# A hybrid Hyena/attention/expert block in fp32: absolute values of the filters written to SBUF, the input projection's casts and evictions early in the program's order, the third sine ahead of the products with the norm

## The chip, the core and the metric

The kernel runs on one core of one Trainium2 chip. The metric is the time of one execution in device microseconds (us); for a version it is the median of several runs.

## What is computed

One encoder layer on a sequence of L = 1024 tokens with D = 1024 channels, batch 1, all in fp32. The reference, cut to what matters here:

```python
mod = silu(c) @ w_ada + b_ada                  # sh1, sc1, gt1, sh2, sc2, gt2
h = rms_norm(x, g_mix) * (1 + sc1) + sh1
z = h @ w_in + b_in                            # -> hyena v, x1, x2 | q | k | v | branch gates
# filters: a three-layer sine MLP 33 -> 64 -> 64 -> 64 on the position, then w4
hdn = sin(fr[0] * (pos @ w1 + b1)); hdn = sin(fr[1] * (hdn @ w2 + b2)); hdn = sin(fr[2] * (hdn @ w3 + b3))
f = (hdn @ w4) * exp(-t * abs(deltas)); f = f / (sum(abs(f), axis=0) + EPS)
y = v                                          # hyena: short 3-tap convolution of z first
for o in range(2):
    y = gates[o] * (bidir_fftconv(y, f[:, o, 0], f[:, o, 1]) + fb[o] * y)
o = softmax(rope(norm(q)) @ rope(norm(k)).T) @ v       # 8 heads, 2 of them for keys and values
x = x + gt1 * ((sigmoid(g_hy) * (y @ w_hy_out) + sigmoid(g_at) * (o @ w_att_out)) @ w_out)
x = x + gt2 * expert_choice_ffn(rms_norm(x, g_ffn) * (1 + sc2) + sh2)   # 16 SwiGLU experts
```

## The kernel before

**Arithmetic.** TensorE multiplies in a fast fp32 form ("fp32r"), so a product of full accuracy is three products of high and low parts, a_h b_h + a_h b_l + a_l b_h: `mm3`, L145 to L147. A high part is a cast on ScalarE, a low part a subtraction on VectorE. For a block of weights that pair is `wsplit`: cast wh at L140, residual wl at L141, from a raw tile wr that SyncE loads.

**Stages.** Times are those of the profiled execution.

- 0 to 60 us, the head. ScalarE and VectorE compute the norm of x and the three sine layers; `sine` is the range reduction on VectorE (L226 to L232, tile wf), `sin` the table function on ScalarE. VectorE multiplies the eight tiles of x by the norm; this is "the products with the norm". `by_rows` (L246) is the product of silu(c) with w_ada for shift1, and `columns` turns its row into columns with two copies (L252, tile z) and 16 tiny products (L255). The third layer's sine stands behind the products with the norm, its casts (tiles Hs, sh) behind it. All this runs in `in_order()`, which chains the instructions of each engine in the order of the code. At its end `shifted` (L361, L363) applies scale and shift to x, and casts and residuals make hT, the input of the input projection (L367, L369, L373).
- 60 to 117 us, the filters: `filters(0)`, `filters(1)`. For each, the weights w4 are cast (L269) and reduced to the residual (L270). Eight times: four products per filter tile into PSUM tile pS (L280), times the decay (VectorE, L284; the decay itself is ScalarE's L274), the absolute value with a running sum on ScalarE (L285), whose result goes back into pS and isn't read, and then the normalisation (L290) and a store to DRAM, k_s.
- 117 to 358 us, `spectra(0)` and `spectra(1)`. `plane` loads a plane of a filter (tile xg, L441), `tokens` transposes it on TensorE (L447), `split2` makes high and low parts (L428, L429: sh, sl), and `dft` multiplies it by constants that `load_const` fetches on the queue of POOL (tile dc, L434). An 8-point FFT on VectorE (`fft8`) combines the planes.
- Then rotary q, k and v, written to DRAM (QT_s, KT_s, V_s), and `hyena_in(0)` to `hyena_in(11)`: the projection blocks of the hyena inputs with the three taps (L417) and a store.
- 358 to 635 us, the two convolutions, chained through generators: forward transform, product with the spectrum, `inverse` (casts Zh, Zl at L671, L672), gate; in the second one the result is transposed and gated (L717) and stored to y_s.
- From 635 us attention: `scores` (products, maximum L793, exponential L795), `turned` (transposes L804, casts L808, L809: ph, pl), `values`, and as filler between them `hyena_out`, which loads y_s (tile yq, L850), splits it (L852, L853: yh, yl) and multiplies by w_hy_out. Then merge and output projection (to about 1050 us), routing and the experts (to the end).

**The input projection** is 34 blocks of 128 columns, `win_block(m)`: 0 to 11 hyena, 12 to 17 q, k, v (their eviction is L553, tile ge), 18 to 33 gates. Each is 48 products in two halves, into PSUM tile pM, and an eviction `evac` on ScalarE.

**What sets the order.** Each engine carries out its queue in order. The queues are filled by a list scheduler: among instructions whose producers it holds done, the one with the lowest priority number is next. The number is a counter, `tc.cur_priority`, that grows with the code, so code that is written early is placed early. `lane(n)` gives the projection's products numbers from 1,000,000 n on, which makes them fillers: they are taken where nothing else is ready. Their casts, residuals and evictions had numbers of their place in the code.

**Buffers.** Tiles of one tag share a number of buffers: f4 9, z4 3, Z 4 (decays, zt, Zh, Zl, QT), dc 3, xg 2, H 2 (here the times t01, later the loaded spectra), wr, wh, wl, sh, sl, wf, ge and yq 2 each; PSUM pS, pT, pM 2 each. A tile can be written when the last reader of that buffer is done. SyncE issues most transfers, POOL those of dc and the first loads of QT, KT, V.

Of the kernel before, what the change touches and what calls it, by code (L numbers as in the profile page):

```python
# [51 lines left out]
def block(tc, xT, cols_d, rows_d, mlp_d, w4_d, dfc_d, idf_d, rope_d, wada_d, win_d, why_d, watt_d, wout_d, wr_d,  # L52
# [133 lines left out]
    def mixer_head():  # L186
# [11 lines left out]
        def z4(shape=(128, 1024), dt=F32):  # L198
            return wk.tile(list(shape), dt, name="z4", tag="z4", bufs=3)
# [65 lines left out]

        def filters(o):

            w4h, w4l = z4(dt=F32R), z4(dt=F32R)
            nc.scalar.copy(w4h, w4r[o])  # L269
            nc.vector.tensor_sub(w4l, w4r[o], w4h)  # L270
            sums = rn[:, o * 8:o * 8 + 8].rearrange("p (b r) -> p b r", r=2)
            for b in range(4):
                dec = wk.tile([128, 1024], F32, name="dec", tag="Z", bufs=4)
                nc.scalar.activation(dec, t01b, AF.Exp, scale=col("ndel", b))  # L274
                ts = []
                for dr in range(2):
                    m = dr * 4 + b
                    ps = pS()
                    for hf in range(2):
                        mm(ps[:, hf], w4h[:, m * 128:(m + 1) * 128], Hs[hf], start=True, stop=False)  # L280
                        mm(ps[:, hf], w4l[:, m * 128:(m + 1) * 128], Hs[hf], start=False, stop=True)
                    t = f4([128, 1024])
                    pf = ps.rearrange("p a b -> p (a b)")
                    nc.vector.tensor_mul(t, pf, dec)  # L284
                    nc.scalar.activation(pf, t, AF.Abs, accum_out=sums[:, b, dr:dr + 1])  # L285
                    ts.append(t)
                nc.vector.tensor_scalar(sums[:, b], sums[:, b], EPS, None, op0=ALU.add)
                nc.vector.reciprocal(sums[:, b], sums[:, b])
                for dr, t in enumerate(ts):
                    nc.scalar.activation(t, t, AF.Copy, scale=sums[:, b, dr:dr + 1])  # L290
                    nc.sync.dma_start(k_s[o, dr, b], t.rearrange("p (q t) -> p q t", q=8))
# [8 lines left out]
        with in_order():  # L300
# [30 lines left out]
                                    rr[:, q:q + 1].to_broadcast([128, 128]), ident)  # L331
            for k in range(4, 8):
                adaln(acc, stage[1][k], k)
            for k in range(8):
                nc.vector.tensor_mul(xt[k], xt[k], rb.rearrange("p a b -> p (a b)"))
            prow = [pT([1, 512]) for hf in range(2)]
# [2 lines left out]
                if k == 2:  # L339
                    mod_cols(acc, 1, pM)  # L340
            nc.vector.scalar_tensor_tensor(G1, modc[:, 8:16], 1.0, col("g_mix", 0, 8), op0=ALU.add, op1=ALU.mult)
            h = sine(p3, "b3", "f3")
            sin(h)
            up, low = slice(64, 128), slice(0, 64)
            t = w2("sh", dt=F32R)
            Hs += [hsp.tile([128, 512], F32R, name=f"Hs{hf}") for hf in range(2)]
            nc.scalar.copy(Hs[0][low], h[low])
            nc.scalar.copy(t[up], h[up])
            nc.vector.tensor_sub(Hs[0][up], h[low], Hs[0][low])
            nc.vector.tensor_sub(Hs[1][up], h[up], t[up])  # L350
            first = wsplit(first)
            pg = columns(prow)
            nc.scalar.copy(Hs[1][low], h[up])
            nc.vector.tensor_add(modc[:, 0:8], pg, col("b_ada", 0, 8))
            sx.close()
            hpool = hx.enter_context(tc.tile_pool(name="hT", bufs=1, side="right", reuse_waits="tile"))
# [9 lines left out]
            for k in range(0, 8, 2):  # L366
                nc.scalar.copy(hTh[k], xt[k])  # L367
                shifted(k + 1)
                nc.scalar.copy(hTh[k + 1], xt[k + 1])  # L369
                if k < 6:  # L370
                    shifted(k + 2)
                for i in (k, k + 1):
                    nc.vector.tensor_sub(hTl[i], xt[i], hTh[i])  # L373
        filters(0)
        if "Hs" in dbg:
            for hf in range(2):
# [7 lines left out]


        def win_block(m, evac, n=0):
            wh, wl = first if m == 12 else wsplit(wload(win_d[m]))

            def step(ps, sl, k):
                ks = slice(k * 128, k * 128 + 128)  # L390
                mm3(ps, (wh[:, ks], wl[:, ks]), (hTh[k][:, sl], hTl[k][:, sl]), k == 0, k == 7)
            halves = [slice(hf * 512, hf * 512 + 512) for hf in range(2)]
            if m == 12:

                ps = [pM() for sl in halves]
                for k in range(8):
                    for hf, sl in enumerate(halves):
                        step(ps[hf], sl, k)
                for hf, sl in enumerate(halves):
                    evac(ps[hf], sl)  # L400
                return
            for sl in halves:
                ps = pM()
                with lane(n) if n else ExitStack():
                    for k in range(8):
                        step(ps, sl, k)
                evac(ps, sl)

        def hyena_in(m, n=0):
            z = z4([128, 8, 128])  # L410
# [19 lines left out]
            return h, l  # L430

        def load_const(src):
            t = w2("dc", [128, 2, 256], F32R, 3)
            nc.gpsimd.dma_start(t, src)  # L434
            return t


        def plane(src, q, spare=False):

            t = z4([128, 4, 128]) if spare else w2("xg", [128, 4, 128])  # L440
            nc.sync.dma_start(t, src[:, :, q].rearrange("b p c -> p b c"))  # L441
            return t

# [1014 lines left out]
```

## Time and profile before

| | |
|---|---|
| median of 3 runs | 2263.3 us (2262.97 to 2269.51) |
| profiled execution | 2261.93 us, its span 2260.1 us |
| mean granted TensorE clock | 0.979 |
| PE (TensorE matmul) | 2129.1 us busy, 94% of the span, 10090 instructions |
| PEld (weight loads, beside PE) | 1686.4 us, 75% |
| DVE (VectorE) | 1886.3 us, 83% |
| ACT (ScalarE) | 1303.9 us, 58% |
| POOL (GpSimd) | 118.2 us, 5% |
| HBM | 538.60 MB read, 65.01 MB written |

The span goes from the first to the last instruction; 1.8 us of the execution lie around it. Shares are averages over very different stages: over half of the span is the experts, which the change doesn't touch. A row of a group reads: line, engine, operation, output <- inputs, partitions x elements; then busy time and mean ns, and the idle time of the engine just before them with what ended it. A row of the timeline begins with start and length in us; in square brackets stands the wait before it and what released it. A row of the table of stages gives each engine's busy time and number of instructions in a stretch; PEclk is TensorE's granted clock as a share of the full one.

### The profile page before, as it was taken

What the parts mean: (1) busy time and instruction counts of PE and PEld (TensorE: products, weight loads), DVE (VectorE), ACT (ScalarE), POOL (GpSimd) and SP (SyncE); (2) the same over time, 40 slices, a digit from 0 to 9 for tenths busy, and PEclk for the clock granted to TensorE, in tenths of its full rate; (3) what the DMA queues carried; (4) which work ended last, traced back from release to release, by engine and by line L of the source; (5) the groups of instructions that cost most, each with busy time, mean ns of one, the idle gap of its engine ahead of it and who ended that gap; (6) DMA issues with size and microseconds to landing.
All of it is one profiled execution on the core that took longest, in us unless ns stands there. A gap on an engine that the chain in (4) does not pass through costs nothing. (4 is left out here: it accounts for less than half of the span.)

```text
span 2260.1 us, 26964 instructions
## 1 busy us (share of the span) xinstructions
PE 2129.1 (94%) x10090; PEld 1686.4 (75%) x10090; DVE 1886.3 (83%) x2117; ACT 1303.9 (58%) x1422; POOL 118.2 (5%) x127
## 2 busy tenths in 40 slices
PE   5799999999999999998699999999999999999997
PEld 1567878878778888775577777777778787787776
DVE  7657787998988888644789888898988989889986
ACT  3942454232376664213477766677677677677674
POOL 0011000000000000002100010000000000000000
PEclk9799999999999999998799999999999999999999
DMA  7378655554453224667599999999999999999994
GB/s 294 144 220 265 236 180 171 181 153 146 136 191 116 84 75 133 226 227 277 205 365 365 370 358 324 376 365 377 362 354 380 368 375 357 362 373 368 379 324 149
DMA packets 157190, 605.38 MB, mean 268 GB/s; under 512 B 14466, under 2 KB 51586, under 8 KB 107780
## 3 DMA queue, kind: packets, MB, share of 16 engines
q1 hardware_dynamic: 141364, 562.77, 66.7%
q0 software_dynamic: 15696, 40.90, 7.0%
q8 instruction: 79, 1.29, 0.2%
q14 instruction: 51, 0.42, 0.1%
HBM read 538.60 MB, written 65.01 MB: 267 GB/s over the span
## 5 line engine op out<-in xcount | busy, mean ns | idle before, releaser
L1178 DVE TENSOR_TENSOR el<-raw,eh 128x2048 fp32r<-128x2048 f32 (+1 forms) x451 | 861.2, 1945 | 62.7 <-ACT eh L1177 60.1
L1177 ACT CAST eh<-raw 128x2048 fp32r<-128x2048 f32 (+1 forms) x456 | 721.2, 1641 | 59.9 <-PE py L147 29.8
L146 PE MATMUL pM<-el,xh 128*128 128x512 f32 x1024 | 406.1, 397 | 8.7 <-DVE el L1178 8.6
L145 PE MATMUL pM<-eh,xh 128*128 128x512 f32 x1024 | 406.4, 397 | 7.9 <-ACT eh L1177 6.1
L147 PE MATMUL pM<-eh,xl 128*128 128x512 f32 x1024 | 401.6, 392 | 0.0
L146 PEld LDWEIGHTS pM<-el,xh 128*128 128x128 f32 x1024 | 192.6, 188 | 62.0 <-DVE el L1178 24.6
L145 PEld LDWEIGHTS pM<-eh,xh 128*128 128x128 f32 x1024 | 192.7, 188 | 50.5 <-ACT eh L1177 8.9
L147 PEld LDWEIGHTS pM<-eh,xl 128*128 128x128 f32 x1024 | 192.8, 188 | 37.8
L146 PE MATMUL pM<-hT,wh 128*128 128x512 f32 x544 | 213.6, 393 | 0.8 <-DVE hT L373 0.8
L145 PE MATMUL pM<-hT,wh 128*128 128x512 f32 x544 | 212.7, 393 | 1.0 <-ACT hT L367 1.0
L147 PE MATMUL pM<-hT,wl 128*128 128x512 f32 x544 | 213.4, 392 | 0.0
L146 PE MATMUL py<-el,hh 128*128 128x512 f32 x512 | 205.5, 401 | 1.4 <-DVE el L1178 1.3
L145 PE MATMUL py<-eh,hh 128*128 128x512 f32 x512 | 202.1, 395 | 1.8 <-ACT hh L1253 1.5
L147 PE MATMUL py<-eh,hl 128*128 128x512 f32 x512 | 200.3, 391 | 0.1
L140 ACT CAST wh<-wr 128x1024 fp32r<-128x1024 f32 (+1 forms) x58 | 54.0, 933 | 171.4 <-PE pM L146 94.5
L145 PEld LDWEIGHTS pM<-hT,wh 128*128 128x128 f32 x544 | 102.3, 188 | 22.2 <-ACT hT L367 1.8
L146 PEld LDWEIGHTS pM<-hT,wh 128*128 128x128 f32 x544 | 102.4, 188 | 21.9 <-DVE hT L373 1.3
L147 PEld LDWEIGHTS pM<-hT,wl 128*128 128x128 f32 x544 | 102.3, 188 | 20.4
L145 PEld LDWEIGHTS py<-eh,hh 128*128 128x128 f32 x512 | 96.5, 188 | 26.4 <-ACT hh L1253 6.0
L146 PEld LDWEIGHTS py<-el,hh 128*128 128x128 f32 x512 | 96.4, 188 | 23.8 <-DVE el L1178 4.7
L147 PEld LDWEIGHTS py<-eh,hl 128*128 128x128 f32 x512 | 96.7, 189 | 19.3 <-DVE hl L1254 0.4
L808 ACT CAST ph<-pM 128x512 fp32r<-128x512 f32 x128 | 74.7, 585 | 54.3 <-PE pM L804 49.0
(367 smaller groups left out, 3389.5 us busy)
## 6 DMA issues: line engine op xcount, KB each, us to landing
raw<-in_wg_dram SPq DMA_DIRECT2D x128, 1024.0 KB, 7.5
raw<-in_wu_dram SPq DMA_DIRECT2D x128, 1024.0 KB, 7.1
raw<-in_wd_dram SPq DMA_DIRECT2D x128, 1024.0 KB, 7.1
wr<-in_win_dram SPq DMA_DIRECT2D x34, 512.0 KB, 3.6
dc<-in_dfc_dram POOLq DMA_DIRECT2D x48, 256.0 KB, 3.7
wr<-in_wada_dram SPq DMA_DIRECT2D x24, 512.0 KB, 4.1
st<-in_wada_dram SPq DMA_DIRECT2D x16, 512.0 KB, 10.0
k_s<-f SPq DMA_DIRECT2D x16, 512.0 KB, 2.7
```

The source lines that it names most:

```text
L140: nc.scalar.copy(h, raw)
L145: mm(o, a[0], b[0], start=start, stop=False)
L146: mm(o, a[0], b[1], start=False, stop=False)
L147: mm(o, a[1], b[0], start=False, stop=stop)
L808: nc.scalar.copy(ph, ps)
L1177: nc.scalar.copy(h[:, ks], raw[:, ks])
L1178: eng.tensor_sub(l[:, ks], raw[:, ks], h[:, ks])
```

## The change

It has four parts.

1. The absolute values (L285) are written to an SBUF tile of tag H instead of the PSUM tile. So that buffers suffice, the second filter's w4l is a tile of tag Z instead of z4.
2. The third sine, its table function and the three casts of Hs stand ahead of the products with the norm.
3. `soon()` is a context whose counter starts right before `filters(0)`, with 10000 numbers set aside. The casts and residuals of the projection's weights and the evictions of its blocks (all blocks but the first's cast) take their numbers from it. They come early among what is ready; the products keep their lanes.
4. dc has 5 buffers instead of 3, xg 3 instead of 2.

```diff
--- before.py
+++ after.py
@@ -265,7 +265,7 @@
 
         def filters(o):
 
-            w4h, w4l = z4(dt=F32R), z4(dt=F32R)
+            w4h, w4l = z4(dt=F32R), zt(F32R) if o else z4(dt=F32R)
             nc.scalar.copy(w4h, w4r[o])
             nc.vector.tensor_sub(w4l, w4r[o], w4h)
             sums = rn[:, o * 8:o * 8 + 8].rearrange("p (b r) -> p b r", r=2)
@@ -282,7 +282,7 @@
                     t = f4([128, 1024])
                     pf = ps.rearrange("p a b -> p (a b)")
                     nc.vector.tensor_mul(t, pf, dec)
-                    nc.scalar.activation(pf, t, AF.Abs, accum_out=sums[:, b, dr:dr + 1])
+                    nc.scalar.activation(w2("H", [128, 1024]), t, AF.Abs, accum_out=sums[:, b, dr:dr + 1])
                     ts.append(t)
                 nc.vector.tensor_scalar(sums[:, b], sums[:, b], EPS, None, op0=ALU.add)
                 nc.vector.reciprocal(sums[:, b], sums[:, b])
@@ -331,6 +331,14 @@
                                     rr[:, q:q + 1].to_broadcast([128, 128]), ident)
             for k in range(4, 8):
                 adaln(acc, stage[1][k], k)
+            h = sine(p3, "b3", "f3")
+            sin(h)
+            up, low = slice(64, 128), slice(0, 64)
+            t = w2("sh", dt=F32R)
+            Hs += [hsp.tile([128, 512], F32R, name=f"Hs{hf}") for hf in range(2)]
+            nc.scalar.copy(Hs[0][low], h[low])
+            nc.scalar.copy(t[up], h[up])
+            nc.scalar.copy(Hs[1][low], h[up])
             for k in range(8):
                 nc.vector.tensor_mul(xt[k], xt[k], rb.rearrange("p a b -> p (a b)"))
             prow = [pT([1, 512]) for hf in range(2)]
@@ -339,18 +347,10 @@
                 if k == 2:
                     mod_cols(acc, 1, pM)
             nc.vector.scalar_tensor_tensor(G1, modc[:, 8:16], 1.0, col("g_mix", 0, 8), op0=ALU.add, op1=ALU.mult)
-            h = sine(p3, "b3", "f3")
-            sin(h)
-            up, low = slice(64, 128), slice(0, 64)
-            t = w2("sh", dt=F32R)
-            Hs += [hsp.tile([128, 512], F32R, name=f"Hs{hf}") for hf in range(2)]
-            nc.scalar.copy(Hs[0][low], h[low])
-            nc.scalar.copy(t[up], h[up])
             nc.vector.tensor_sub(Hs[0][up], h[low], Hs[0][low])
             nc.vector.tensor_sub(Hs[1][up], h[up], t[up])
             first = wsplit(first)
             pg = columns(prow)
-            nc.scalar.copy(Hs[1][low], h[up])
             nc.vector.tensor_add(modc[:, 0:8], pg, col("b_ada", 0, 8))
             sx.close()
             hpool = hx.enter_context(tc.tile_pool(name="hT", bufs=1, side="right", reuse_waits="tile"))
@@ -371,6 +371,16 @@
                     shifted(k + 2)
                 for i in (k, k + 1):
                     nc.vector.tensor_sub(hTl[i], xt[i], hTh[i])
+        head = [tc.cur_priority]
+        tc.cur_priority += 10000
+
+        @contextmanager
+        def soon():
+
+            keep, tc.cur_priority = tc.cur_priority, head[0]
+            yield
+            head[0], tc.cur_priority = tc.cur_priority, keep
+
         filters(0)
         if "Hs" in dbg:
             for hf in range(2):
@@ -384,7 +394,12 @@
 
 
         def win_block(m, evac, n=0):
-            wh, wl = first if m == 12 else wsplit(wload(win_d[m]))
+            if m == 12:
+                wh, wl = first
+            else:
+                raw = wload(win_d[m])
+                with soon():
+                    wh, wl = wsplit(raw)
 
             def step(ps, sl, k):
                 ks = slice(k * 128, k * 128 + 128)
@@ -397,14 +412,16 @@
                     for hf, sl in enumerate(halves):
                         step(ps[hf], sl, k)
                 for hf, sl in enumerate(halves):
-                    evac(ps[hf], sl)
+                    with soon():
+                        evac(ps[hf], sl)
                 return
             for sl in halves:
                 ps = pM()
                 with lane(n) if n else ExitStack():
                     for k in range(8):
                         step(ps, sl, k)
-                evac(ps, sl)
+                with soon():
+                    evac(ps, sl)
 
         def hyena_in(m, n=0):
             z = z4([128, 8, 128])
@@ -430,14 +447,14 @@
             return h, l
 
         def load_const(src):
-            t = w2("dc", [128, 2, 256], F32R, 3)
+            t = w2("dc", [128, 2, 256], F32R, 5)
             nc.gpsimd.dma_start(t, src)
             return t
 
 
         def plane(src, q, spare=False):
 
-            t = z4([128, 4, 128]) if spare else w2("xg", [128, 4, 128])
+            t = z4([128, 4, 128]) if spare else w2("xg", [128, 4, 128], bufs=3)
             nc.sync.dma_start(t, src[:, :, q].rearrange("b p c -> p b c"))
             return t
```

Lines of the new kernel are shifted: L553 is L570, L717 is L734, L793 is L810, L808 is L825, L853 is L870. In the order of TensorE's instructions, 169 products of the projection now stand ahead of the first spectrum product, 48 before. From a place within attention on, every engine's order is the same in both. Three places of the order follow, of before and of the new one; a number behind a name tells tiles apart.

ScalarE in the second half of the first filter and the start of the second, before:

```order
L285 ACTIVATE pS_409,rn_80<-f4_414 128x1024
L285 ACTIVATE pS_425,rn_80<-f4_430 128x1024
L290 ACTIVATE f4_406<-f4_406,rn_80 128x1024
L290 ACTIVATE f4_414<-f4_414,rn_80 128x1024
L285 ACTIVATE pS_433,rn_80<-f4_438 128x1024
L274 ACTIVATE dec_447<-H_164,cols_71 128x1024
L290 ACTIVATE f4_430<-f4_430,rn_80 128x1024
L290 ACTIVATE f4_438<-f4_438,rn_80 128x1024
L285 ACTIVATE pS_449,rn_80<-f4_454 128x1024
```

and in the new order:

```order
L285 ACTIVATE H_436,rn_80<-f4_434 128x1024
L570 ACTIVATE ge_1399<-pM_1349,cols_71 128x512
L570 ACTIVATE ge_1402<-pM_1350,cols_71 128x512
L140 CAST wh_1469<-wr_1467 128x1024
L290 ACTIVATE f4_408<-f4_408,rn_80 128x1024
L290 ACTIVATE f4_417<-f4_417,rn_80 128x1024
L285 ACTIVATE H_445,rn_80<-f4_443 128x1024
L269 CAST z4_479<-X_162 128x1024
L290 ACTIVATE f4_434<-f4_434,rn_80 128x1024
L570 ACTIVATE ge_1436<-pM_1411,cols_71 128x512
```

Evictions (ge), a weight cast (wh) and the cast of the second filter's w4 (z4) now stand between the filters' instructions; before, the first ge stood behind the last decay, and the next weight cast behind the second cast of the spectra.

VectorE at the end of the head, before, from the last instruction of the third sine:

```order
L232 TENSOR_SCALAR wf_292<-wf_292 128x512
L561 TENSOR_SCALAR gain_1701<-gain_1701 128x64
L349 TENSOR_TENSOR Hs0_303<-wf_292,Hs0_303 64x512
L350 TENSOR_TENSOR Hs1_304<-wf_292,sh_302 64x512
L141 TENSOR_TENSOR wl_310<-wr_159,wh_309 128x1024
L354 TENSOR_TENSOR modc_73<-pM_316,cols_71 128x8
L363 TENSOR_SCALAR f4_127<-f4_127,G1_74,modc_73 128x1024
L363 TENSOR_SCALAR f4_129<-f4_129,G1_74,modc_73 128x1024
L270 TENSOR_TENSOR z4_372<-X_161,z4_371 128x1024
```

and in the new order, from behind the products with the norm:

```order
L172 TENSOR_TENSOR modc_73<-pM_287,cols_71 128x8
L270 TENSOR_TENSOR z4_372<-X_161,z4_371 128x1024
L349 SCALAR_TENSOR_TENSOR G1_74<-modc_73,cols_71 128x8
L350 TENSOR_TENSOR Hs0_266<-wf_255,Hs0_266 64x512
L351 TENSOR_TENSOR Hs1_267<-wf_255,sh_265 64x512
L141 TENSOR_TENSOR wl_311<-wr_159,wh_310 128x1024
L354 TENSOR_TENSOR modc_73<-pM_317,cols_71 128x8
L284 TENSOR_TENSOR f4_382<-pS_377,dec_375 128x1024
L363 TENSOR_SCALAR f4_127<-f4_127,G1_74,modc_73 128x1024
L363 TENSOR_SCALAR f4_129<-f4_129,G1_74,modc_73 128x1024
```

The sine has gone ahead (wf_255 is its result), and the first filter's product with its decay (f4_382) now stands in front of the two `shifted`.

VectorE at the end of the convolutions and the start of attention, before (z_3743, z_3772 and z_3796 are the last gated planes, z_3759, z_3788 and z_3812 in the new order):

```order
L717 TENSOR_TENSOR z_3743<-pT,z_3743 128x512
L672 TENSOR_TENSOR Zl<-f_3299,Zh 128x1024
L793 TENSOR_REDUCE rs<-pS 128x1
L717 TENSOR_TENSOR z_3772<-pT,z_3772 128x512
L793 TENSOR_REDUCE rs<-pS 128x1
L141 TENSOR_TENSOR wl<-wr,wh 128x512
L717 TENSOR_TENSOR z_3796<-pT,z_3796 128x512
L793 TENSOR_REDUCE rs<-pS 128x1
L809 TENSOR_TENSOR pl<-pM,ph 128x512 x2
```

and in the new order:

```order
L734 TENSOR_TENSOR z_3759<-pT,z_3759 128x512
L689 TENSOR_TENSOR Zl<-f_3315,Zh 128x1024
L734 TENSOR_TENSOR z_3788<-pT,z_3788 128x512
L734 TENSOR_TENSOR z_3812<-pT,z_3812 128x512
L164 TENSOR_SCALAR acc<-wr,siluc 128x1024
L166 SCALAR_TENSOR_TENSOR acc<-wr,siluc,acc 128x1024
L870 TENSOR_TENSOR yl<-yq,yh 128x4x128 x4
L810 TENSOR_REDUCE rs<-pS 128x1 x2
L166 SCALAR_TENSOR_TENSOR acc<-wr,siluc,acc 128x1024
```

The first maxima of the scores (rs, L793, now L810) stood among the last gated planes; now four residuals yl of `hyena_out` and two steps of the adaLN row (acc) stand between those planes and the maxima.

## The prediction

> **What bounds the kernel now.** I read the table of stages first, then the waits inside the stages that the change reaches, then the instructions in order of time at the ends of each stage. The boundaries are places in the program: 60.6 is the first filter product, 117 the first spectrum product, 358 the first product of the convolutions, 474 the first inverse transform of the first convolution, 603 that of the second, and 635 the end of the convolutions, where attention takes over.
>
> ```profile
> core 0: us, PE busy (x) PEld busy (x) DVE busy (x) ACT busy (x) POOL busy (x), PEclk, DMA share, GB/s
> 60.00:117.00 57.00, 38.58 (x125) 26.92 (x124) 36.87 (x49) 52.63 (x68) 0.00 (x0) 0.74 0.41 157
> 117.00:358.00 241.00, 234.24 (x1098) 186.89 (x1098) 179.71 (x261) 99.97 (x143) 16.89 (x32) 0.99 0.66 219
> 358.00:474.00 116.00, 115.73 (x521) 94.42 (x520) 105.41 (x132) 35.70 (x46) 4.22 (x8) 1.00 0.54 173
> 474.00:603.00 129.00, 123.61 (x552) 100.35 (x550) 118.46 (x145) 40.72 (x55) 8.44 (x16) 1.00 0.47 141
> 540.00:600.00 60.00, 60.00 (x266) 49.69 (x266) 59.72 (x76) 12.85 (x17) 0.00 (x0) 1.00 0.43 141
> 603.00:635.00 32.00, 26.89 (x123) 20.39 (x124) 26.86 (x34) 16.95 (x24) 5.30 (x10) 0.95 0.68 218
> 635.00:680.00 45.00, 42.05 (x271) 35.79 (x270) 42.34 (x59) 33.74 (x62) 0.53 (x1) 1.00 0.50 167
> ```
>
> The reader is to see four things. The filter stage (60 to 117) is ScalarE's: 52.6 of 57 us busy, while TensorE has 18 us free and runs at a mean clock of 0.74. From 117 to 474 TensorE is full. From 540 to 600 TensorE and VectorE are both full, but TensorE's work there is nearly all input-projection blocks, which fill holes; VectorE carries the chain. And 266 products in 60 us price one product at 0.226 us.
>
> ```profile
> PE pS L280 <- ACT pS L285: 8.6, 5, 2.1
> PE pS L280 <- ACT z L269: 4.9, 1, 4.9
> PE pS L145 <- ACT sh L428: 3.0, 1, 3.0
> ```
>
> These are TensorE's waits in the filter stage: for the absolute values to release PSUM, for a cast of the second filter's weights that needs a buffer, and for ScalarE's first spectrum cast.
>
> **The head, up to the first filter product.**
>
> ```profile
> 45.55 0.80 DVE L226 TENSOR_SCALAR wf<-pM,cols 128x512 f32<-128x512 f32 x1
> 49.49 0.43 DVE L232 TENSOR_SCALAR wf<-wf 128x512 f32<-128x512 f32 x1
> 41.79 8.74 PE L246 MATMUL pT<-st,siluc 128*1 128x512 f32 x20
> 56.50 1.04 ACT L252 COPY z<-pT 1x512 f32<-1x512 f32 x2
> 57.12 3.57 PE L255 MATMUL pM<-ones,z 1*128 1x1 f32 x16 [6.59 <-ACT z L252]
> 60.62 1.22 PE L280 MATMUL pS<-Hs,z 128*128 128x512 f32 x2
> 60.93 1.54 DVE L363 TENSOR_SCALAR f<-f,G,modc 128x1024 f32<-128x1024 f32 x2
> 61.78 1.05 ACT L367 CAST hT<-f 128x1024 fp32r<-128x1024 f32 x1 [2.53 <-DVE f L363]
> ```
>
> The third sine takes VectorE 45.55 to 49.92, 4.4 us, behind the products with the norm. Ahead of them it delays those products by 4.4 us, which nobody is waiting for yet: the row products of L246 end at 50.5 in both kernels. What it frees is ScalarE, whose sine, casts and table load stood before the copies at 56.50. In the new order the copies stand around one cast (0.5 + 1.0 + 0.5), so they end at 52.4, L255 ends at 56.0, and the filter products start 4.6 us earlier. But VectorE now has the first filter's product with its decay (L284) ahead of the first L363. It waits for four products at the cold rate (0.43 us each, twice 0.226), until 58.3, and takes 1.2. The first L363 ends at about 60.2, so the cast of hT is only 1.6 us earlier.
>
> **The filter stage.** ScalarE sets its length.
>
> ```profile
> L290 ACT ACTIVATE f<-f,rn 128x1024 f32<-128x1024 f32 x15 | 16.4, 1136 | 0.5 <-DVE rn L288 0.5
> L285 ACT ACTIVATE pS<-f 128x1024 f32<-128x1024 f32 x16 | 16.1, 1009 | 2.1 <-DVE rn L288 0.9 <-DVE rn L287 0.9 <-DVE f L284 0.3
> L285 ACT ACTIVATION_READ_ACCUMULATOR pS<-f 128x1 f32 x16 | 3.0, 187 | 0.0
> 116.49 0.80 PE L145 MATMUL pS<-sh,dc 128*128 128x512 f32 x1 [2.97 <-ACT sh L428]
> 119.01 0.69 ACT L553 ACTIVATE ge<-pM,cols 128x512 f32<-128x512 f32 x1
> 119.59 1.99 ACT L140 CAST wh<-wr 128x1024 fp32r<-128x1024 f32 x2
> ```
>
> Between the first hT cast and the first spectrum cast, the new order has five more evictions (0.6 each, start to start) and three more weight casts (1.0), and two decays fewer, since those now run while ScalarE used to wait: 3.0 + 3.0 - 2.2 = +3.8 us. The absolute values move from PSUM to SBUF. No row has that form, so I bound it by L285 itself (1009 ns to PSUM, no change) and by L290 (1136 ns, SBUF to SBUF): 0 to 2.0 us over 16, and I take 1.0, in the middle, as both differ from it in one thing. The Trainium skill's page "ScalarE: Activation LUTs" (Step-by-step: what each stage is for) says that ScalarE reaches PSUM faster than SBUF and advises PSUM as destination; it speaks against this edit, by it the end at 2.0 us would hold, and the total would be 1 us longer. On the other side PSUM is released by VectorE instead of ScalarE, and TensorE's 8.6 us of waits go. The stage's start is 1.6 us earlier, and I let half a microsecond of ScalarE's own waits go. The first spectrum product moves from 116.5 to 116.5 - 1.6 + 3.8 + 1.0 - 0.4 = 119.3, that is 2.8 us later.
>
> By then TensorE has done more. In the new order 169 projection products stand ahead of the first spectrum product, 48 before: 121 more, 27.3 us. At its first spectrum product TensorE is thus 27.3 - 2.8 = 24.5 us ahead in work. This is the whole stock; the rest asks how much of it reaches the end. The new order takes these 121 products out of four later stretches: 12 from 117 to 358, 30 from 358 to 474, 55 from 474 to 603, 24 from there to the end of the convolutions.
>
> **The later stretches.** Boundaries and waits:
>
> ```profile
> 358.54 0.50 PE L145 MATMUL pS<-sh,dc 128*128 128x512 f32 x1
> 473.69 0.50 PE L145 MATMUL pT<-Zh,dc 128*128 128x512 f32 x1 [0.20 <-ACT Zh L671]
> 603.05 0.50 PE L145 MATMUL pT<-Zh,dc 128*128 128x512 f32 x1 [0.28 <-ACT Zh L671]
> PE pT L145 <- DMA dc<-in_idf_dram: 5.2, 5, 2.1
> PE pT L447 <- DMA xg<-k_s: 4.5, 6, 1.8
> PE pS L787 <- DMA KT<-KT_s: 2.6, 1, 2.6
> L417 DVE SCALAR_TENSOR_TENSOR z<-z,cols,z 128x896 f32<-128x896 f32 x24 | 27.5, 1144 | 2.3 <-ACT z L414 2.1
> L141 DVE TENSOR_TENSOR wl<-wr,wh 128x1024 fp32r<-128x1024 f32 x42 | 51.2, 1221 | 6.6 <-ACT wh L140 6.0
> ```
>
> 117 to 358: TensorE is full, so its work counts. 12 products are 2.7 us; the clock of 0.99 is 2.4 us that a TensorE warm from the filter stage does not lose; the third buffer of xg can take 0 to 4.5 us of waits, and I take 2.2. Against the late start of 2.8: 2.7 + 2.4 + 2.2 - 2.8 = 4.5 us earlier at 358 (1 to 7).
> 358 to 474: 30 products are 6.8 us for a full TensorE. VectorE has 105.4 busy there and loses four large taps (4.6 us) and a weight residual (1.2), so it doesn't become the bound at once; some waits will show, so I take 5.5. Earlier by 10.
> 474 to 603: 55 products would be 12.4 us, but VectorE is busy 118.5 of 129 and loses one residual (1.2). Only the waits between can go; the five buffers of dc can take up to 5.2 us of them. Between 0 and 6.4 I take 3.5. Earlier by 13.5.
> 603 to 635: the score products and two reductions (1.2 us each) no longer stand inside the last inverse transforms, nor does the 2.6 us wait for KT. Some of it is on the chain: 3 of 5. The convolutions end 16.5 us earlier (9 to 24).
>
> **What is late next.** The price is at the start of attention.
>
> ```profile
> 629.66 1.22 DVE L793 TENSOR_REDUCE rs<-pS 128x1 f32<-128x1024 f32 x1
> 631.35 1.11 ACT L795 ACTIVATE P<-pS,rs 128x1024 f32<-128x1024 f32 x1
> 634.13 0.69 DVE L717 TENSOR_TENSOR z<-pT,z 128x512 f32<-128x512 f32 x1 [0.93 <-PE pT L447]
> 634.82 0.58 ACT L808 CAST ph<-pM 128x512 fp32r<-128x512 f32 x1 [0.69 <-PE pM L804]
> 635.27 1.15 SPq L850 DMA_DIRECT2D yq<-y_s x2
> 641.49 0.62 ACT L852 CAST yh<-yq 128x512 fp32r<-128x512 f32 x1 [1.49 <-DMA yq<-y_s]
> DMA to landing us min/median/max: 2.5/2.7/6.4
> ```
>
> Now the first exponential runs 3.5 us before the convolutions end (634.8), and the first cast of turned probabilities (L808) right at that end. In the new order the first reduction of scores stands behind four residuals yl (L853, L870 in the new numbering), and ScalarE's table load behind the four casts yh. Their loads yq can only be issued after the last store of the convolutions, and yq has two buffers, so the third load waits for the first residual. From the end e: issue 0.4, landing 2.7 (the last row is yq's), cast 0.6, residual 0.7, so 4.4; a second round with two other loads in between, 9; two reductions, 11.5; exponentials and a transpose, 13. The first L808 moves from e to e + 13. VectorE, 42.3 of 45 busy from 635 to 680, sets the pace there: it stands idle some 9 us of these 13, has two reductions (2.4) to make up, and used to idle 2 in this place. Cost: 9 to 13, I take 10. Everything from there on has the same order in both kernels.
>
> The sum against the profiled execution of 2261.9 us: -16.5 + 10 = -6.5, so 2255.4; I say 2255. That execution is 1.4 us below the median of the runs, 2263.3. Forecast case: 2249 to 2260.
>
> **Rivals.** First, all of TensorE's 24.5 us arrive. For it: TensorE is full in every row from 117 to 603. Against: at 540 to 600 VectorE is just as full. If the end of the convolutions is 24 us earlier and attention starts only 4 to 8 late, the time is 2242 to 2246.
> Second, no change: the idle time is only moved. The spectra start 2.8 us later, the chain through 474 to 603 is VectorE's, and only some 9 us arrive, which the late attention takes back: 2262. For it: 118.5 and 59.72 in the table. Against: the full TensorE from 117 to 474.
> Third, slower: the two rounds of yq loads take 6.4 each, the longest in the row, instead of 2.7, because the stores and loads of that place share the queues (the cast at 641.49 did wait that long). The cost is then 17 instead of 10. It decides where the cost exceeds the gain by 7: with the second rival's 9 us the time is 2270, with my 16.5 it is still 2262.
>
> **Chances.** A difference within 0.3%, 6.8 us, is about what a measurement of this kernel can't tell from no change. Forecast 0.48 (of it two thirds below 2256.5), first rival 0.17, second 0.22, third 0.13. Faster: 0.32 + 0.17 = 0.49; slower: the third and a little of the second, 0.15; same 0.36. The range, 2243 to 2267, leaves out half of the first and two thirds of the third.
>
> **What would show it.** Right: evictions and weight casts in the filter stage, TensorE's clock near 1 there, its waits for L285 gone; the first spectrum product near 119, the first inverse transform near 464, that of the second convolution near 590, the end of the convolutions near 618, and then a hole of about 10 us on TensorE before the first L808. Wrong: a spectrum stage that starts after 122, a first inverse transform that isn't earlier than 470, or no hole at the start of attention.

## The result, and the profile after

The new kernel takes 2250.84 us (median of 8 runs, 2246.23 to 2256.24); the kernel before, in 8 runs, 2263.14. The ratio is 0.9941, with a 95% interval of 0.9922 to 0.9960: 9 to 18 us faster. Its profiled execution has a span of 2249.1 us, 11.0 less than before.

The table of stages of the new kernel, in the columns and stretches of the one before:

```profile
60.00:117.00 57.00, 55.59 (x243) 43.83 (x244) 35.80 (x49) 56.75 (x76) 0.53 (x1) 1.00 0.60 222
117.00:358.00 241.00, 233.62 (x1096) 188.04 (x1096) 184.57 (x270) 98.49 (x141) 17.37 (x33) 0.99 0.67 220
474.00:603.00 129.00, 112.51 (x494) 90.28 (x493) 123.25 (x152) 40.72 (x53) 10.56 (x20) 0.93 0.46 142
603.00:635.00 32.00, 16.53 (x84) 12.64 (x83) 20.85 (x26) 15.57 (x27) 0.54 (x1) 0.79 0.75 256
635.00:680.00 45.00, 44.95 (x301) 39.80 (x300) 40.64 (x57) 33.30 (x59) 1.58 (x3) 1.00 0.25 83
```

In the filter stage TensorE is now as full as ScalarE (55.6 and 56.8 of 57 us), at the full clock instead of 0.74. From 474 on it has holes. The instructions in order of time, at the same boundaries as in the prediction:

```profile
50.04 1.05 PE L255 MATMUL pM<-ones,z 1*128 1x1 f32 x8
51.34 1.15 PE L255 MATMUL pM<-ones,z 1*128 1x1 f32 x8 [0.25 <-ACT z L252]
52.90 0.80 PE L280 MATMUL pS<-Hs,z 128*128 128x512 f32 x1 [0.41 <-DVE Hs L350]
57.72 1.03 ACT L367 CAST hT<-f 128x1024 fp32r<-128x1024 f32 x1
113.80 0.40 PE L145 MATMUL pS<-sh,dc 128*128 128x512 f32 x1
353.52 0.50 PE L145 MATMUL pS<-sh,dc 128*128 128x512 f32 x1
461.36 0.50 PE L145 MATMUL pT<-Zh,dc 128*128 128x512 f32 x1
581.90 0.80 PE L145 MATMUL pT<-Zh,dc 128*128 128x512 f32 x1 [10.01 <-ACT Zh L688]
612.61 0.69 DVE L734 TENSOR_TENSOR z<-pT,z 128x512 f32<-128x512 f32 x1 [3.23 <-DMA z<-hz_s]
628.77 0.59 ACT L825 CAST ph<-pM 128x512 fp32r<-128x512 f32 x1 [0.86 <-PE pM L821]
```

Earlier than before by 2.7 us at the first spectrum product, 5.0 at the start of the convolutions, 12.3 at the first inverse transform, 21.1 at that of the second convolution, 21.5 at the end of the convolutions; then only 6.1 at the first cast of turned probabilities, 12.3 at the 32nd (682.5), and 10.1 at the first cast of the experts (1045.8, before 1055.9). Between the end of the convolutions and the first cast of turned probabilities lies the start of attention, which gives up most of what the stages ahead had won. Its instructions in order of time:

```profile
616.47 0.62 ACT L869 CAST yh<-yq 128x512 fp32r<-128x512 f32 x1 [6.38 <-DMA yq<-y_s]
621.58 0.69 DVE L870 TENSOR_TENSOR yl<-yq,yh 128x512 fp32r<-128x512 f32 x1 [2.69 <-ACT yh L869]
623.30 2.35 DVE L810 TENSOR_REDUCE rs<-pS 128x1 f32<-128x1024 f32 x2
```

TensorE's waits from 600 to 640 (us in total, times, longest):

```profile
PE pS L804 <- ACT P L812: 13.2, 1, 13.2
```

The maxima stand behind four residuals yl, these behind their loads, and TensorE waits 13.2 us for the first exponential.

### The profile page after: what moved, and what is told of

Its sections match the earlier page's. It is cut to its first block, busy times and chain, and to the rows that moved or that the text cites. A ratio compares the mean times of both kernels' runs of the same rounds, so it can differ in the third digit from the quotient of the medians.

```text
span 2249.1 us, 26971 instructions
## 1 busy us (share of the span) xinstructions
PE 2123.5 (94%) x10090; PEld 1687.4 (75%) x10090; DVE 1886.3 (84%) x2117; ACT 1302.1 (58%) x1421; POOL 118.2 (5%) x127
## 5 line engine op out<-in xcount | busy, mean ns | idle before, releaser
L147 PEld LDWEIGHTS py<-eh,hl 128*128 128x128 f32 x512 | 96.7, 189 | 19.2 <-DVE hl L1271 0.4
L825 ACT CAST ph<-pM 128x512 fp32r<-128x512 f32 x128 | 74.7, 585 | 55.6 <-PE pM L821 51.7
```

Of the source, the lines that this page charges most:

```text
L147: mm(o, a[1], b[0], start=False, stop=stop)
L825: nc.scalar.copy(ph, ps)
```

## The experiments

All start from the new kernel or from that before; ratios are to the kernel before, with 95% intervals. The table gives, from each profile, in us, the start of the first spectrum product, then three stretches: from there to the first inverse transform, on to the first one of the second convolution, and on to the first cast ph of attention; then when that cast and the first cast of the experts start. The profiled execution of these kernels lies between 5.5 us below the median of its runs (only_soon; no_bufs 4.9, no_sine 3.0) and 2.0 above it (scores_acc), so rows of the table that differ by a few us don't rank two kernels; for that the ratios are there.

| kernel | first spectrum | + to first inverse | + to second conv.'s inverse | + to first ph | first ph | experts |
|---|---|---|---|---|---|---|
| before | 116.5 | 357.2 | 129.4 | 31.8 | 634.8 | 1055.9 |
| new | 113.8 | 347.6 | 120.5 | 46.9 | 628.8 | 1045.8 |
| only_soon (part 3) | 122.4 | 358.9 | 125.3 | 30.6 | 637.2 | 1056.3 |
| only_sine (part 2) | 106.3 | 360.1 | 128.5 | 31.9 | 626.9 | 1048.1 |
| no_soon (1, 2, 4) | 106.5 | 356.7 | 123.2 | 45.6 | 632.0 | 1048.5 |
| no_sine (1, 3, 4) | 124.3 | 351.3 | 120.5 | 48.8 | 645.0 | 1059.5 |
| no_bufs (1, 2, 3) | 115.1 | 356.1 | 124.5 | 32.1 | 627.8 | 1047.8 |
| no_abs (2, 3, 4) | 115.7 | 342.8 | 120.5 | 48.7 | 627.6 | 1044.3 |
| scores_acc (all four, maxima first) | 114.6 | 344.6 | 120.5 | 37.5 | 617.2 | 1042.8 |

**Is it the early products?** Part 3 of the change's diff alone, on the kernel before.

> Only part 3 (soon) on the kernel before: absolute values in PSUM, sine in its old place, dc 3 and xg 2 buffers. Theory A (the gain is TensorE's early products, so part 3 alone carries most of it): 171 products stand ahead of the first spectrum product; without the earlier head that product is at 118 to 121 us, the end of the convolutions is 14 to 19 us earlier than in the kernel before (634.8), and the time is 2251 to 2256. Theory B (the earlier head, the released PSUM and the added buffers carry most): end of the convolutions 3 to 9 us earlier and, since the late start of attention costs 10 as before, 2261 to 2268.

Measured: 2264.36 us, ratio 1.0001 (0.9988 to 1.0013). 171 products stand ahead of the first spectrum product, and on balance nothing of them arrives. Theory A falls; the time is theory B's, though at the end of the convolutions it is even 2.2 us later than before. TensorE's waits from the first spectrum product to the convolutions:

```profile
PE pT L464 <- DMA xg<-k_s: 8.0, 7, 2.9
PE pT L598 <- DMA X<-zq_s: 6.4, 1, 6.4
```

These are 14 us, against 4.5 and 0.4 before. My reading, not tested by itself: a TensorE with less filler comes to its loads too early. And the start itself is 5.9 later. A part of that is order: the cast of the first filter's w4 stands behind the first hT cast (63.94; before it stood ahead of it, 58.21), so the filter products start at 65.9 instead of 60.6. From the first spectrum product to the first ph only_soon is 3.6 us shorter than the kernel before, so even without the late start little of the 27 us would have arrived.

The converse, the new kernel with an empty `soon()`:

```diff
-            keep, tc.cur_priority = tc.cur_priority, head[0]
             yield
-            head[0], tc.cur_priority = tc.cur_priority, keep
```

> The new kernel without part 3 (parts 1, 2 and 4 alone). Theory A: the first spectrum product comes at 109 to 112 us, since ScalarE has no projection work in the filter stage, but the 121 products are still to be made later; TensorE is full, so at most these 5 to 7 us are earlier at the end of the convolutions, attention starts as in the kernel before, and the time is 2255 to 2261. Theory B: end of the convolutions 12 or more earlier, 2252 or less.

Measured: 2252.37 us, ratio 0.9941 (0.9923 to 0.9959), the same as the new kernel. The end of the convolutions is at 615.6, 19.2 earlier than before: theory B, within half a microsecond of its time. With only the 48 early products of the kernel before it is as fast. Theory A's first spectrum product was expected at 109 to 112 and came at 106.5.

**Which part is it, then?** The new kernel with the sine put back:

The diff is cut:

```diff
-            h = sine(p3, "b3", "f3")      # and sin(h), the three casts: ahead of
-            ...
             for k in range(8):
                 nc.vector.tensor_mul(xt[k], xt[k], rb.rearrange("p a b -> p (a b)"))
...
+            h = sine(p3, "b3", "f3")      # back behind G1, as in the kernel before
+            ...
```

> The new kernel without part 2 (third sine behind the products with the norm). Theory C: the first hT cast, 57.7 in the new kernel, comes at 61 to 62, the first spectrum product at 117 to 118 instead of 113.8, the end of the convolutions 3 to 4 us later, time 2254 to 2255. Rival: 187 instead of 169 projection products ahead of the first spectrum product make up for it: 2250 to 2252.

Measured: 2266.73 us, ratio 1.0010 (0.9997 to 1.0023). The whole gain is gone, four times what theory C gave it. The first hT cast was placed rightly (61.7), the first spectrum product not: 124.3, 10.5 us later than in the new kernel. As in only_soon, a second weight cast now stands ahead of the first hT cast, the cast of the first filter's w4 behind it, and the filter products start at 65.8 (new kernel 52.9):

```profile
58.16 1.04 ACT L140 CAST wh<-wr 128x1024 fp32r<-128x1024 f32 x1
61.72 1.04 ACT L367 CAST hT<-f 128x1024 fp32r<-128x1024 f32 x1 [2.52 <-DVE f L363]
63.82 1.02 ACT L269 CAST z<-X 128x1024 fp32r<-128x1024 f32 x1
```

The sine alone, on the kernel before:

> Only part 2 (the third sine ahead of the products with the norm) on the kernel before. Theory D (the early sine lets ScalarE work where it sat idle behind the sine's range reduction, so the ScalarE-bound filter stage ends earlier, and this start is what arrives): first spectrum product at 108 to 113 instead of 116.5; waits for dc and xg as before; end of the convolutions at 627 to 631; attention starts there without a lag, as dc has 3 buffers; time 2255 to 2260. Rival (the sine helps only together with part 3's early products): first spectrum product at 114 or later, time 2261 to 2266.

Measured: 2253.85 us, ratio 0.9948 (0.9931 to 0.9965): its interval and the new kernel's overlap almost wholly. The first spectrum product is at 106.3, 1.7 us below theory D's range, and the time 1 us below it; from there to the first ph the stretches are those of the kernel before (+2.9, -0.9, +0.1 in the table; TensorE's waits for xg are 7.5 us instead of 4.5), so 7.9 of the 10.1 us arrive. Where they come from: two of ScalarE's waits in the head of the kernel before, the first for the load of the times (H), the second for the sine's range reduction,

```profile
41.32 1.15 ACT L274 ACTIVATE dec<-H,cols 128x1024 f32<-128x1024 f32 x1 [10.75 <-DMA H<-in_rows_dram]
49.99 1.28 ACT L236 ACT_TABLE_LOAD   x1 [7.53 <-DVE wf L232]
```

and the engines' busy time from 40 us to the first hT cast, and on to the first spectrum product, of the kernel before:

```profile
40.00:61.80 21.80, 15.21 (x54) 7.35 (x54) 13.41 (x21) 10.29 (x13) 0.00 (x0) 0.81 0.23 80
61.80:116.50 54.70, 36.28 (x120) 25.54 (x119) 35.33 (x47) 52.12 (x68) 0.00 (x0) 0.75 0.41 156
```

and of only_sine:

```profile
40.00:57.30 17.30, 15.26 (x54) 6.97 (x53) 15.41 (x19) 13.16 (x15) 0.00 (x0) 0.90 0.27 98
57.30:106.30 49.00, 36.23 (x112) 24.39 (x112) 31.92 (x42) 46.55 (x63) 0.00 (x0) 0.76 0.42 156
```

ScalarE's instructions of only_sine in that place (cut):

```profile
40.21 1.28 ACT L236 ACT_TABLE_LOAD   x1 [11.40 <-DVE wf L232]
...
52.23 4.27 ACT L274 ACTIVATE dec<-H,cols 128x1024 f32<-128x1024 f32 x4
56.40 1.03 ACT L269 CAST z<-X 128x1024 fp32r<-128x1024 f32 x1
```

and its last two normalisations of the filters, first before, then in only_sine:

```profile
116.45 2.19 ACT L290 ACTIVATE f<-f,rn 128x1024 f32<-128x1024 f32 x2
110.88 2.19 ACT L290 ACTIVATE f<-f,rn 128x1024 f32<-128x1024 f32 x2
```

Ahead of the first hT cast ScalarE was busy 10.3 of 21.8 us, now 13.2 of 17.3. It still waits for the sine's range reduction, 11.4 us, but until 40.21, in time in which before it waited 10.75 us for H. The second wait, 7.53 us, is gone, so four decays and both casts of w4 are done by the first hT cast, where before it was two decays and one cast. The stage behind it has less left to do, 46.6 instead of 52.1 us ahead of the first spectrum product. Not all of that is saved: four normalisations and one absolute value of the filters stand behind that product in only_sine, two normalisations before. ScalarE's last normalisation ends 5.6 us earlier (113.07, before 118.64), with some 2 us of other work more ahead of it (an eviction, a weight cast and a spectrum cast), so some 4.5 of the 10.1 us are order. What arrives, 7.9 us, fits the wait that is gone: hidden idle time of the engine that bounds the next stage was the gain.

**The buffers.** Two sizes of the new kernel put back:

```diff
-            t = w2("dc", [128, 2, 256], F32R, 5)
+            t = w2("dc", [128, 2, 256], F32R, 3)
...
-            t = z4([128, 4, 128]) if spare else w2("xg", [128, 4, 128], bufs=3)
+            t = z4([128, 4, 128]) if spare else w2("xg", [128, 4, 128])
```

> The new kernel without part 4 (dc 3, xg 2 buffers). In its order the first maxima stand among the last gated planes again, as in the kernel before, so attention should start at the end of the convolutions. Theory C (the added buffers carry a part of the gain, since only_soon lost 14 us to waits for xg and X in the spectra and the rotations): waits for xg of 6 to 10 us and for dc of 1 to 5 come back, the first product of the convolutions is at 357 to 366 instead of 353.5, the end of the convolutions at 619 to 627, the time 2250 to 2258. Rival (the buffers do nothing but change the order at attention): end of the convolutions at 613 to 615, time 2240 to 2244.

Measured: 2256.12 us, ratio 0.9961 (0.9948 to 0.9973), theory C, though the end of the convolutions is 0.8 above its range. The first product of the convolutions is at 361.5, their end at 627.8, 14.5 later than in the new kernel; waits of TensorE from the first spectrum product to the first inverse sum to 14.3 us, against 7.0:

```profile
PE pT L464 <- DMA xg<-k_s: 6.1, 7, 2.4
PE pT L598 <- DMA X<-zq_s: 3.1, 1, 3.1
PE pT L464 <- DMA xg<-hz_s: 1.5, 1, 1.5
```

But attention starts at once (627.8), within 1 us of the new kernel's 628.8. Every kernel of the table with dc at 3 starts it 30.6 to 32.1 us behind the second convolution's first inverse, and every one with dc at 5 and no further edge in the order 45.6 to 48.8: part 4 wins 14.5 us up to the end of the convolutions, and the order that it brings about at attention costs nearly as much. Which of the two tags does what was not separated. In total the profile has part 4 at 2 us (1047.8 against 1045.8), the ratios at 4.5, and the intervals of the ratios overlap: its share is not settled.

**The absolute values.** Back into PSUM, in the new kernel:

```diff
-            w4h, w4l = z4(dt=F32R), zt(F32R) if o else z4(dt=F32R)
+            w4h, w4l = z4(dt=F32R), z4(dt=F32R)
...
-                    nc.scalar.activation(w2("H", [128, 1024]), t, AF.Abs, ...)
+                    nc.scalar.activation(pf, t, AF.Abs, ...)
```

> The new kernel without part 1 (absolute values into PSUM, w4l in z4). Theory C (the filter stage's length is the whole chain's start, and freeing PSUM by VectorE shortens it): the filter stage from the first hT cast to the first spectrum product, 56.1 us in the new kernel, 54.7 before and 48.1 in no_soon, becomes 59 to 63; the first spectrum product is at 117 to 121 and the end of the convolutions 3 to 6 us later than 613.3; time 2253 to 2257. Rival: ScalarE's own work sets the stage, where PSUM or SBUF costs it nothing: 0 to 1 us later, 2250 to 2252.

Measured: 2250.84 us, ratio 0.9938 (0.9922 to 0.9955): no share at all in the time, as the rival said, though the filter stage is longer (57.8 us from the first hT cast, against 56.1), less than theory C gave it. What it is behind there, 1.9 us, it has made up at the first inverse transform, 2.9 ahead.

**The start of attention.** One edge in the order of the new kernel:

```diff
-                nc.scalar.copy(yh[:, :, sl], t)
+                behind(nc.scalar.copy(yh[:, :, sl], t), exps[5])     # order only, no wait
```

> The new kernel with one more edge in the order: the casts yh of the hyena output stand behind the sixth exponential, so the residuals yl no longer stand ahead of the first score maxima. Theory A (the 10 us lost at the start of attention are the maxima's wait behind yl and their loads): TensorE's 13.2 us hole at 612 to 626 shrinks to 4 or less, the first cast of turned probabilities moves from 628.8 to 615 to 619, and the time is 5 to 9 us below the new kernel's 2250.8, 2242 to 2246. Rival: VectorE's work is the bound there (42.3 of 45 us busy before), and the fillers wait for yh and yl instead: 2249 to 2252.

Measured: 2255.48 us, ratio 0.9950 (0.9935 to 0.9965), no gain, outside both ranges, and the first cast ph at 631.1. The hole stayed (11.2 us), since a step acc of the adaLN row, written in `hyena_out` too, stood ahead of the maxima:

```profile
624.17 1.28 DVE L166 SCALAR_TENSOR_TENSOR acc<-wr,siluc,acc 128x1024 f32<-128x1024 f32 x1 [6.59 <-DMA wr<-in_wada_dram]
625.38 2.35 DVE L810 TENSOR_REDUCE rs<-pS 128x1 f32<-128x1024 f32 x2
```

So this run did not test theory A. With the same edge for these steps:

```diff
-                adaln(acc, wload(wada_d[2, m]), m)
+                behind(adaln(acc, wload(wada_d[2, m]), m), exps[5])
```

> As scores_first (the casts yh behind the sixth exponential), and the steps acc of the adaLN row behind it as well: in scores_first the first maxima stood behind one such step, which waited 6.6 us for its weights, queued behind the loads of yq. Theory A (what is lost at the start of attention is VectorE's order there): TensorE's hole of 13.2 us in the new kernel (11.2 in scores_first) shrinks to 4 or less, the first cast of turned probabilities comes at 615 to 620, and the time is 2242 to 2247. Rival (the time lost there is given back anyway within the next 40 us, because VectorE has the same work to do): the cast comes early but the 32nd cast not, and the time is 2249 to 2253.

Measured: 2246.37 us, ratio 0.9910 (0.9892 to 0.9928). The maxima follow the last gated plane at once, and of the hole 3.5 us are left:

```profile
612.75 2.35 DVE L810 TENSOR_REDUCE rs<-pS 128x1 f32<-128x1024 f32 x2
617.16 0.59 ACT L825 CAST ph<-pM 128x512 fp32r<-128x512 f32 x1 [0.83 <-PE pM L821]
```

```profile
PE pS L804 <- ACT P L812: 4.2, 2, 3.5
```

The first cast is 11.6 us earlier than in the new kernel, the 32nd 3.4, the experts 3.0. So both were right in part: the order makes the hole, and about a quarter of the lead stays; the rest is given back in the next 50 us.

**The last planes.** Planes 5, 3 and 7 of the last gate in xg and ge, whose last readers seemed done:

```diff
-                    g = chan(2, r, r not in (0, 1))
+                    g = chan(2, r, "ge" if r in (3, 7) else r not in (0, 1, 5) and "z4")
```

> The new kernel with the planes of the last gate in other tiles (planes 5, 3 and 7 in xg and ge, whose last users are done, instead of z4), so that their loads do not wait for stores of y. The new kernel's VectorE waits 1.8 and 3.2 us for the last two of these planes. Theory A: the end of the convolutions, 613.3 in the new kernel, comes 4 to 5 us earlier, and as the loads of yq hang on its last store, the time follows: 2246 to 2247. Rival: the chain of the last inverse transforms (each 2.8 to 3 us: copy, transpose, product) is next: 1 to 3 us earlier, 2248 to 2250.

Measured: 2410.61 us, ratio 1.0646 (1.0622 to 1.0671), outside both ranges, a miss of mine. As I read the order, the ring of ge orders its users as the code does, and the gates' evictions are written behind the planes, so 720 projection products, 15 blocks, moved behind the second convolution's first inverse, nearly all of them behind the end of the convolutions, where VectorE has little to do (the second row). It tells one thing: with TensorE busy 34 us only VectorE still needs 114.7 us between the first inverse transforms (the first row).

```profile
455.10:569.80 114.70, 34.45 (x124) 24.30 (x124) 108.87 (x137) 20.90 (x27) 8.45 (x16) 0.65 0.28 80
600.00:700.00 100.00, 98.80 (x423) 81.55 (x424) 9.80 (x8) 21.10 (x28) 0.00 (x0) 0.97 0.28 95
```

**Combinations.** scores_acc with planes 5, 3, 7 in xg alone (`chan(2, r, r in (4, 2, 6))`):

> scores_acc with the last gate's planes 5, 3 and 7 in xg (3 buffers) instead of z4, so that their loads do not queue behind stores of y. VectorE waited 1.8 and 3.2 us for such loads in the new kernel. Theory: end of the convolutions 3 to 5 us before scores_acc's 612.8, of which 2 to 4 arrive: 2242 to 2244. Rival: the chain of copy, transpose and gate is next: 0 to 1 us, 2245 to 2247.

Measured: 2244.99 us, ratio 0.9904 (0.9888 to 0.9920); end of the convolutions 611.6, 1.2 earlier, less than expected, and nearer to the rival. scores_acc without part 3, and without part 1:

> Parts 1, 2 and 4 (no_soon) with the order at attention of scores_acc. Theory D: end of the convolutions at 614 to 617 as in no_soon, first cast of turned probabilities at 619 to 622 instead of 632, and of that lead 3 to 5 us arrive: 2247 to 2250. If part 3 has no share of its own at the end, this equals scores_acc (2246.4) within 2 us.

> Parts 2, 3 and 4 (no_abs) with the order at attention of scores_acc. no_abs was as fast as the new kernel, so this is as fast as scores_acc: 2245 to 2248. If the absolute values in SBUF do have a share that the start of attention hid, it is slower: 2249 to 2252.

Measured: 2246.62 us, 0.9925 (0.9907 to 0.9942), and 2246.33, 0.9919 (0.9906 to 0.9932). The first equals scores_acc within 2 us, so part 3 has no share of its own that the times show; the second is as fast too. The four kernels with the maxima first can't be told apart by their times; 0.9904 is the lowest ratio of all. Against the new kernel's 0.9941 their intervals overlap too, so it is the profiles (experts at 1038 to 1043 instead of 1045.8) that speak for 3 to 7.5 us.

## Why the prediction held, and where its working did not

The time lies in the forecast case (2249 to 2260), 4 us under the single figure. Much of the working was wrong in size, and its main step in cause; that the total came so near is partly luck.

- **The stock.** The prediction took the gain from "121 more, 27.3 us": products that TensorE has done when the spectra start. This step failed. Part 3 alone makes 123 and gains nothing; without it the time is the same. What part 3 does is in the table: in the filter stage it costs 7.3 us (113.8 against 106.5), in the next two stretches it gives back 9.1 and 2.7, and the last takes 1.3: 3.2 us by the first ph, which the times don't show. The new kernel's end of the convolutions, 21.5 us earlier, comes near the 24 of the first rival, but not by the stock: no_soon's is 19.2 earlier. That rival fails on the late start of attention, 15.5 us instead of 4 to 8. What lets no more of the stock through shows between the inverse transforms: all four kernels of the table with parts 3 and 4 have 120.5 us there, with TensorE waiting 10 us at the end. VectorE, busy 117.4 of these 120.5 us, is the bound, as the prediction said of 540 to 600. The stretch, before and in the new kernel:

```profile
473.69:603.05 129.36, 123.92 (x553) 100.62 (x553) 118.82 (x147) 41.08 (x55) 8.44 (x16) 1.00 0.47 141
461.36:581.90 120.54, 110.52 (x499) 90.41 (x498) 117.36 (x147) 38.77 (x51) 8.44 (x16) 0.97 0.47 146
```

- **The sine.** Its share at the first spectrum product was put at 3.8 us: 1.6 by which the first hT cast is earlier, and 2.2 for two decays that run where ScalarE waited. It is 10.1 alone and 10.5 within the new kernel, and the sine is the whole of the gain that the times show. The term that failed is the 1.6, which came out as 4.1. The 16 tiny products L255 were taken at their old 3.6 us; with the wait of 6.59 ahead of them gone they took 1.05 and 1.15. The copies ended at 51.3, not 52.4, since the first ran at 49.29, when only the first half of the row was done (the products of the row end at 50.1). So the filter products started at 52.9, not 56.0. The two decays were right for the new kernel. Not in the working was what part 3 costs without part 2: the cast of w4 behind the first hT cast, and filter products at 65.8. And some of the 10 us are instructions of the filters that now stand behind the first spectrum product. The wait that the early sine removes, ScalarE's 7.53 us behind L232, is in none of the prediction's rows.
- **The filter stage** was forecast at 119.3 and came at 113.8: 2.5 us from the earlier hT, 1.9 from ScalarE's waits (2.6 us before, 0.3 after; I had taken off 0.4), 1.0 from the absolute values. That last term had the wrong sign within the new kernel, whose first spectrum product is 1.9 us earlier than no_abs's. L285 went from 1009 to 1048 ns, yet from one start to the next, read-out included, it is 1.04 us in both. The Trainium skill's rule (page "ScalarE: Activation LUTs", section "Step-by-step: what each stage is for") that ScalarE is slower to SBUF has the sign of these 39 ns; by the times of no_abs it made no difference.
- **Spectra to convolutions** should have won 7.3 us and won 2.3. The two terms that failed are the clock (0.99 in both) and xg's waits (4.5 before, 4.6 after). The convolutions up to the first inverse won 7.3 instead of 5.5, and the last stretch, to the end of the convolutions, 0.4 instead of 3. Between the inverse transforms it won 8.8 instead of 3.5: the 5.2 us of waits for dc vanished whole (no_soon, with 5 dc buffers and without part 3, wins 6.2 there), and part 3 added 2.7.
- **The start of attention** went the way that was forecast, in mechanism too: maxima behind four yl, a hole (about 10 forecast, 13.2 measured), first cast at e + 15.5 instead of e + 13. Its cost to the experts, 21.5 less 10.1, is 11.4; forecast 10. The third rival's loads of 6.4 us did not occur: the first yq was issued at 613.70 and its cast ran at 616.47; all eight landed within 2.7 to 3.7 us.
- **The sum** came out near because errors met. Against the forecast the new kernel is 5.5 us better at the first spectrum product, 5.0 worse up to the convolutions, 1.8 and 5.3 better in the next two stretches and 2.6 worse in the last: 5.0 better at their end. Attention takes back 11.4 instead of 10. The size is nearly right, but the gain was put on the wrong part.

What stays open: scores_acc has the maxima first and still loses 8.8 us between the end of the convolutions (22.0 earlier than before) and the experts (13.2). The kernel before had made its first two maxima and an exponential by its end of the convolutions; whether that accounts for it was not tried.

## What to carry to other kernels

An engine that is idle ahead of a stage which it bounds is worth looking at early: let what it waits for come first, even where another engine is busy then, and put two of its waits into the same time. Work done early on another engine is worth only what the bound of each later stage lets through; add up stretch by stretch, and test a change of several parts by leaving each out, since here one part of four carried the time, and what the buffers won was nearly taken back by the order that came with them. A buffer added for one wait may reorder a place far behind it: look there too.

## What had not been expected of the hardware

The 16 products L255 of one row took 3.57 us behind a wait of 6.59 us, at a granted clock of 0.50 from 57.1 to 60.6, and 2.2 us when TensorE had just been busy, at 0.93 from 50.0 to 52.5. So here the lower clock behind the wait was part of what the wait cost.
